# Output projection and gate of a hybrid decoder layer as seven quadrant products per pair of token tiles

## The chip, the cores and the metric

One core of a Trainium2 chip. The metric is the device time of one execution in microseconds; given is the median of three runs. The profile is of one further execution. TensorE (PE) does the matrix products, VectorE (DVE), ScalarE (ACT) and GpSimd (POOL) everything else; SyncE (SP) and the queue of ACT issue the transfers. Each engine works off its own instructions in program order.

## The reference

One decoder layer over 2048 prompt tokens and 8 x 8 sample tokens, width 1024, all in float32:

```
h   = rms_norm(x) ; z = h @ w_in                       # 1024 -> 3584
a   = silu(gate_A) * u * (W_s layernorm(v) + b)        # spatial gating, 512 wide
b   = silu(gate_B) * groupnorm(retention(q, k, v))     # 4 heads, 512 wide
mix = concat(a, b) @ w_out                             # 1024 -> 1024
x   = x + rms_norm(mix)
x   = x + sigmoid(x @ w_gate) * (p @ w_ple)            # 1024 -> 1024, 256 -> 1024
```

It returns the new x of both token sets, the retention states and the normalised v rows of the sample.

## The kernel before

The prompt is 16 tiles of 128 tokens, the sample one tile of 64. The work runs in five passes over these 17 tiles (sample between tiles 7 and 8): S (u, v and gate of the spatial part, three groups of 512 columns), R twice (two heads each: q and k, then v and gate), C1 (the output projection, two groups of 512 columns) and C2 (the gate, two groups of 512, each followed by the embedding product of the same columns). A main product has 128 features by 128 tokens stationary and 128 by 512 of a weight moving. For float32 accuracy each operand is split into a rounded part (hi) and its remainder (lo), and each chunk of 128 features costs three products, hi-hi, hi-lo and lo-hi; for the sample hi and lo lie side by side in the stationary operand and it costs two. So a C1 tile has 2 x 8 x 3 = 48 main products and a C2 tile 48 + 2 x 2 x 3 = 60.

`Stream` (L53) writes the order of every engine out by hand. It counts the main products issued. After each one `tick()` runs the closures that fall due and steps the generators of side work: a `yield 4` in one means that its next instruction is written down four products later. Where a text says that something stands at product n, it means this place in the program; the engine reaches it when what stands ahead of it on that engine is done.

`weight_pass` and `fill` (L199, L232) load, round (ACT, L214 or L216) and subtract (DVE, L223 or L225) the weights; hi and lo stay in the pool `ring`, 52 slots of 2 KB. The operands of a tile are split by `split_cols` (L242: ACT L251, then DVE or POOL L253) and lie in the pool `big`, ten buffers of 4 KB. Further pools hold the temporaries. A pool gives out again the slot that has been free longest; the first writer waits for the last user of the slot.

Between the passes the activations go through DRAM: a tile is transposed in blocks of 32 by 32 on DVE (`blocks`, L176) and scattered (`scatter`, L183) to `mixT` and `x2T`, from which the next pass loads features by tokens, in runs of 1 KB. In C1 (`post`, L801) two squares on ACT with a sum (L807) give the norm, three small POOL operations its factor (L811, L295, L296), DVE scales straight out of PSUM (L818), POOL adds the residual (L822), and the ACT queue issues the store of x2 and the four parts of its transposed form, five issues a tile. In C2 (L835, L841) ACT takes the tanh of the gate out of PSUM (L838) and DVE combines it with the embedding product, in PSUM too, and with x2 (L850, L853). The main products use four PSUM banks of 512 columns in turn, the side products four others.

In R, POOL rotates q and k (L474, L475, L478), multiplies the gate with the group-norm weights (L504) and works on the group norm (L535 to L537, L546).

Of the kernel before, what the change touches and what calls it, by code (L numbers as in the profile page):

```python
# [12 lines left out]
F32 = mybir.dt.float32  # L13
# [36 lines left out]
F_0 = 10  # L50


class Stream:  # L53
    """Orders the tensor engine: main products, with side work placed between them."""
# [50 lines left out]
def hybrid_step(ctx: ExitStack, tc: tile.TileContext, a: dict):  # L105
# [4 lines left out]
    ring = ctx.enter_context(tc.tile_pool(name="ring", bufs=52))  # L110
    big = ctx.enter_context(tc.tile_pool(name="big", bufs=10))
# [10 lines left out]

    def wtile(shape, dt=F32):
        return ring.tile(shape, dt, tag="W", name=name("W"))

    def vtile(shape, dt=F32):
        return work.tile(shape, dt, tag="v2", name=name("v2"), bufs=8)

    def xtile(shape, dt=F32):
        return big.tile(shape, dt, tag="X", name=name("X"))  # L130

    def t2k(shape, dt=F32):
        return work.tile(shape, dt, tag="t2", name=name("t2"), bufs=10)

    def t1k(shape, dt=F32):
        return work.tile(shape, dt, tag="t1", name=name("t1"), bufs=11)

    def c4k(shape, dt=F32):
        return work.tile(shape, dt, tag="c4", name=name("c4"), bufs=2)
# [27 lines left out]
    x2T = [dram.tile([4 if t < NT else 2, P, KD, 32], F32, name=f"x2T{t}") for t in range(NT + 1)]  # L167
    x2d = [dram.tile([P if t < NT else TS, D], F32, name=f"x2d{t}") for t in range(NT + 1)]
# [7 lines left out]
    def blocks(tile_, src, n):  # L176
        """src [n, 128 * nk] transposed in blocks of 32 by 32, the blocks of one quarter of the features together"""
# [5 lines left out]
    def scatter(dst, src, n, qu=None):  # L183
        """src [n, 4, nk, 32] from blocks() to dst [n / 32, 128, nk, 32] in DRAM: features by tokens"""
# [9 lines left out]
    def mm(out, l, r, start, stop):  # L194
        st.pe = True
        PE.matmul(out, lhsT=l, rhs=r, start=start, stop=stop)  # L196
# [44 lines left out]
    # ------------------------------------------------------- x operands (split)  # L241
    def split_cols(raw, t, eng):  # L242
# [6 lines left out]
        if len(raw.shape) == 4:  # L249
            hi, lo = (o.rearrange("p k (a r) -> p a k r", r=32) for o in (hi, lo))  # L250
# [647 lines left out]
    def length(u):  # L898
        if u.first:
            return 216  # L900
# [178 lines left out]
```

## Time and profile before

| | |
|---|---|
| median of 3 runs | 1148.37 us (1147.71 to 1148.89) |
| span of the profiled execution, first to last instruction | 1146.2 us |
| PE busy | 1139.0 us, 99% |
| DVE, ACT, POOL busy | 53%, 30%, 38% |
| mean transfer rate | 138 GB/s |

The profile gives for the profiled execution its span; the runs are timed from outside and their median lies 2.2 us above it. Busy time of PE is the time covered by its records, which overlap each other at their ends.

### The profile page before, as it was taken

What the parts mean: (1) busy time and instruction counts of PE and PEld (TensorE: products, weight loads), DVE (VectorE), ACT (ScalarE), POOL (GpSimd) and SP (SyncE); (2) the same over time, 40 slices, a digit from 0 to 9 for tenths busy, and PEclk for the clock granted to TensorE, in tenths of its full rate; (3) what the DMA queues carried; (4) which work ended last, traced back from release to release, by engine and by line L of the source; (5) the groups of instructions that cost most, each with busy time, mean ns of one, the idle gap of its engine ahead of it and who ended that gap; (6) DMA issues with size and microseconds to landing.
All of it is one profiled execution on the core that took longest, in us unless ns stands there. A gap on an engine that the chain in (4) does not pass through costs nothing.

```text
span 1146.2 us, 15123 instructions
## 1 busy us (share of the span) xinstructions
PE 1139.0 (99%) x5316; PEld 943.1 (82%) x5316; DVE 604.7 (53%) x1094; ACT 346.5 (30%) x648; POOL 436.3 (38%) x621
## 2 busy tenths in 40 slices
PE   9999999999999999999999999999999999999998
PEld 7888878888888888788888887888888888888886
DVE  4866575566745655675456457643344652233332
ACT  6543433335312322242123123412222421112110
POOL 6654434533334465653444575443334210000000
PEclk9999999999999999999999999999999999999999
DMA  9343123124353442663443427656666763335431
GB/s 312 98 146 96 40 73 119 39 85 135 101 159 96 119 110 81 189 184 97 117 121 95 117 70 213 212 193 191 202 228 227 240 221 120 108 111 150 131 106 55
DMA packets 140300, 157.75 MB, mean 138 GB/s; under 512 B 30656, under 2 KB 106688, under 8 KB 140224
## 3 DMA queue, kind: packets, MB, share of 16 engines
q1 hardware_dynamic: 128336, 139.48, 39.9%
q10 hardware_dynamic: 11888, 17.31, 4.8%
q8 instruction: 42, 0.69, 0.3%
q14 instruction: 34, 0.28, 0.1%
HBM read 110.99 MB, written 45.74 MB: 137 GB/s over the span
## 4 chain that ended last, share of the span: by engine, by line
PE 94%; DMA 2%; POOL 2%; DVE 1%; SPq 1%; issue 0%; ACT 0%; DVEq 0%; ACTq 0%; POOLq 0%
PE z L196 87%; PE s L196 7%; DMA W<-w_in 1%; DMA X<-x 1%; POOL v L377 1%; POOL t L361 0%; SPq L920 0%; DMA X<-sguT 0%; POOL X L253 0%; SPq L207 0%; DVE ti L351 0%; DVE t L337 0%; DVE t L333 0%; DVE W L225 0%; DVE X L305 0%
## 5 line engine op out<-in xcount | busy, mean ns | idle before, releaser
L196 PE MATMUL z<-W,X 128*128 128x512 f32 x4328 | 1072.6, 396 | 1.6 <-DVE W L225 0.8
L196 PEld LDWEIGHTS z<-W,X 128*128 128x128 f32 x4328 | 804.0, 188 | 164.4 <-issue 2.6
L253 DVE TENSOR_TENSOR X<-X,X 128x1024 fp32r<-128x1024 f32 (+1 forms) x68 | 81.1, 1192 | 36.6 <-PE z L196 16.4
L850 DVE SCALAR_TENSOR_TENSOR t<-t,z 128x512 f32<-128x512 f32 (+1 forms) x33 | 22.2, 672 | 142.1 <-PE z L196 142.1
L251 ACT CAST X<-X 128x1024 fp32r<-128x1024 f32 (+1 forms) x82 | 83.7, 1020 | 32.9 <-issue 22.8
L196 PEld LDWEIGHTS s<-t,t 128*128 128x128 f32 (+1 forms) x400 | 73.6, 186 | 13.1 <-issue 3.1
L196 PE MATMUL s<-t,t 128*128 128x128 f32 (+2 forms) x400 | 76.3, 272 | 0.0
L498 ACT ACTIVATE t<-z,rsall 128x256 f32<-128x256 f32 x32 | 15.2, 476 | 196.4 <-PE z L196 191.9
L180 DVE STREAM_TRANSPOSE t<-t 128x256 f32<-128x256 f32 (+3 forms) x69 | 39.8, 577 | 61.5 <-POOL t L478 42.5
L838 ACT ACTIVATE t<-z 128x512 f32<-128x512 f32 x32 | 19.1, 598 | 170.5 <-PE z L196 167.6
L474 POOL TENSOR_TENSOR t<-t,t 128x256 f32<-128x256 f32 (+1 forms) x34 | 27.3, 802 | 100.4 <-DVE t L471 86.3
L225 DVE SCALAR_TENSOR_TENSOR W<-W,c_npre,W 128x512 fp32r<-128x512 f32 x56 | 44.7, 819 | 19.9 <-ACT W L216 19.8
L822 POOL TENSOR_TENSOR X<-X,t 128x512 f32<-128x512 f32 (+1 forms) x34 | 45.7, 1364 | 18.1 <-DVE t L818 12.0
L196 PE MATMUL z<-W,t 128*128 128x512 f32 x200 | 50.9, 389 | 0.0
L535 POOL TENSOR_TENSOR ti<-ti,c_cols 128x2 f32<-128x2 f32 (+1 forms) x34 | 11.2, 328 | 96.1 <-DVE ti L531 96.1
L504 POOL TENSOR_TENSOR t<-t,gnw 128x256 f32<-128x256 f32 (+1 forms) x34 | 40.1, 1178 | 18.8 <-DVE t L502 18.4
L216 ACT ACTIVATE W<-W,c_npre 128x512 fp32r<-128x512 f32 x56 | 39.1, 719 | 25.7 <-DMA W<-w_in 23.4
L807 ACT ACTIVATE t<-z 128x512 f32<-128x512 f32 x32 | 19.1, 598 | 91.1 <-PE z L196 91.1
L196 PEld LDWEIGHTS z<-W,t 128*128 128x128 f32 x200 | 37.5, 188 | 7.8
L529 DVE BATCH_NORM_STATS2 ti<-s 128x6 f32<-128x128 f32 x64 | 15.8, 288 | 50.3 <-PE s L196 50.3
L377 POOL TENSOR_TENSOR v<-t,v 128x128 fp32r<-128x128 f32 x64 | 31.4, 512 | 23.4 <-ACT v L375 17.7
L253 POOL TENSOR_TENSOR X<-X,X 128x1024 fp32r<-128x1024 f32 (+1 forms) x14 | 32.9, 2353 | 15.7 <-ACT X L251 9.6
(118 smaller groups left out, 1042.5 us busy)
## 6 DMA issues: line engine op xcount, KB each, us to landing
X<-xT SPq DMA_DIRECT2D x45, 512.0 KB, 4.0
X<-x SPq DMA_DIRECT2D x32, 512.0 KB, 5.0
W<-w_in SPq DMA_DIRECT2D x56, 256.0 KB, 4.4
qkT<-t SPq DMA_DIRECT2D x132, 64.0 KB, 2.0
x2T<-c ACTq DMA_DIRECT2D x66, 128.0 KB, 2.6
t<-qkT SPq DMA_DIRECT2D x32, 256.0 KB, 3.0
X<-mixT SPq DMA_DIRECT2D x16, 512.0 KB, 4.4
x2d<-X ACTq DMA_DIRECT2D x16, 512.0 KB, 2.7
```

Of the source, the lines that this page charges most:

```text
L180: V.transpose(out=out.rearrange("p b k r -> p k b r"), in_=src.rearrange("p (k b r) -> p k b r", b=4, r=32))
L196: PE.matmul(out, lhsT=l, rhs=r, start=start, stop=stop)
L216: S.activation(out=hi, in_=raw, func=AF.Copy, scale=sc)
L225: V.scalar_tensor_tensor(out=lo, in0=raw, scalar=sc, in1=f(hi), op0=ALU.mult, op1=ALU.subtract)
L251: S.copy(out=hi, in_=raw)
L253: eng.tensor_tensor(out=lo, in0=raw, in1=f(hi), op=ALU.subtract)
L377: GP.tensor_tensor(out=los[q][:, :, t % 4, :], in0=i, in1=f(o), op=ALU.subtract)
L474: GP.tensor_tensor(out=qk[:, :, 0, :], in0=t1[:, :, 0, :], in1=t2[:, :, 1, :], op=ALU.subtract)
L504: GP.tensor_tensor(out=g, in0=g, in1=ret["gn"][0:n, 256 * pr : 256 * pr + 256], op=ALU.mult)
L807: S.activation(out=junk, in_=src, func=AF.Square, accum_out=acc["a"][:, g : g + 1])
L822: GP.tensor_tensor(out=x2[:, c], in0=x2[:, c], in1=w, op=ALU.add)
L850: V.scalar_tensor_tensor(out=th[g][:, h], in0=th[g][:, h], scalar=1.0, in1=src[:, h], op0=ALU.add, op1=ALU.mult)
```

## The change

C1 and the gate of C2 no longer work tile by tile. `Fast` takes a pair of token tiles as two block rows and halves features and columns. The left operand has the quadrants A11, A12 (first tile, features 0 to 511 and 512 to 1023), A21, A22 (second tile), the weight B11 to B22. Seven products of quadrants, each of 4 chunks by 3 products, give the four results (Winograd's form of Strassen's scheme), 84 main products for what took 96. The sample tile stays with 32 products, from weights that are there (B12 is B11 + T1, so it adds two products).

Each weight now has 28 chunks of hi and lo, 56 slots, in place of 32. Sixteen of the 28 are differences made on POOL (T1 and T3 of two loaded chunks, T2 and T4 of a loaded chunk and the difference before); they are formed in place in the raw chunk, rounded on ACT and subtracted on DVE. POOL makes four sums of operands (S1 to S4) per pair. Products 1, 3 and 5 add into one PSUM bank ("a"), 2 and 4 into another ("c"), and ACT copies the contents out between them; DVE adds the parts.

The embedding product no longer stands beside the gate: `Ple` is a pass of its own between C1 and C2 that writes its result to DRAM (`pleD`), and C2 reads it back. In C1 the sample is last, in C2 first.

Temporaries, weights and operands share one ring of 98 slots of 2 KB; every 4 KB tile is now two of 2 KB, with two loads or operations for one. So the transposed tiles move in runs of 512 B (1 KB before), those of the spatial part in runs of 256 B (512 B before). The pool of 1 KB tiles grows from 11 to 14. The scratch that the program sets aside for descriptors shrinks to 1 KB.

```diff
-    ring = ctx.enter_context(tc.tile_pool(name="ring", bufs=52))
-    big = ctx.enter_context(tc.tile_pool(name="big", bufs=10))
+    ring = ctx.enter_context(tc.tile_pool(name="ring", bufs=SLOTS))     # 98
...
+    PRODUCTS = (("A11", "B11", "a"), ("S1", "T1", "c"), ("S2", "T2", "a"), ("S4", "B22", "c"),
+                ("S3", "T3", "a"), ("A22", "T4", "d"), ("A12", "B21", "b"))
...
+        def combine(dst, x, y, op):
+            GP.tensor_tensor(out=raws[dst], in0=raws[x], in1=raws[y], op=op)
+        for k in range(4):
+            job("B11", k, lambda k=k: raws[0, 0, k], [(0, 0, k)])
+        for k in range(4):
+            job("T1", k, lambda k=k: raws[0, 0, k], [(0, 1, k)],
+                lambda k=k: combine((0, 0, k), (0, 1, k), (0, 0, k), ALU.subtract))
...                                    # T2 the same way; B22 alone; T3, T4 as T1; B21 alone
+    def fast_fill(jobs, counts):
+        for (loads, scales, total, high, low), c in zip(jobs, counts):
+            for fn in loads:
+                st.at(c - 8 - LAG_W, fn)
...
+            if total:
+                st.at(c - 7, total)
+            st.at(c, high)
+            st.at(c + 4, low)
...
+        def total(self, x, y, op):
+            out = slot("sum", [P, 4, 4, 32])
+            GP.tensor_tensor(out=out, in0=x, in1=y, op=op)
+            return out
+        def prep(self):                                   # from 44 products ahead of the pair
...
+            s1 = self.total(r[1, 0], r[1, 1], ALU.add)
+            yield from self.split("A11", r[0, 0])         # ACT rounds, 4 products later DVE subtracts
+            yield 4
+            s2 = self.total(s1, r[0, 0], ALU.subtract)
+            yield 4
+            yield from self.split("S1", s1)
+            s4 = self.total(r[0, 1], s2, ALU.subtract)
+            yield 8
+            yield from self.split("S2", s2)
+            s3 = self.total(r[0, 0], r[1, 0], ALU.subtract)
+            yield 8
...                                                       # S4, S3, A22, A12, 8 products apart
+        def after(self, i, banks):
...
+            if i == 0:
+                copy("m1", "a")                           # ACT, PSUM to SBUF
+            elif i == 1:
+                copy("m5", "c")
+            elif i == 2:
+                copy("u2", "a")
+            elif i == 3:
+                add("u2", "c")                            # DVE, PSUM + SBUF
+                st.start(self.post_(t0, 1, c["u2"]), 3)
+            elif i == 4:
+                copy("u3", "a")
+                add("m5", "a")
+                st.start(self.post_(t1, 1, c["m5"]), 3)
+            elif i == 5:
+                add("u3", "d")
+                st.start(self.post_(t1, 0, c["u3"]), 3)
+            else:
+                add("m1", "b")
+                st.start(self.post_(t0, 0, c["m1"]), 3)
...
+    class Ple:                                            # 12 products a tile, 8 for the sample
...
+                out = slot("P", [P, 512])
+                S.copy(out=out, in_=bank)
+            store(pleD[self.t][:, 512 * g : 512 * g + 512], out[0:n])
...
+    unitsC1 = [Fast(p, tabC1, mixT, c1_post, c1_begin) for p in pairs + [[SAMPLE]]]
+    unitsP = [Ple(t, PleTab()) for t in order]
+    unitsC2 = [Fast(p, tabC2, x2T, c2_post, c2_begin) for p in [[SAMPLE]] + pairs]
...
+        last = begin[unitsR[1][-1]]
+        fast_fill(jobsC1, [last - 10 * (14 - j) for j in range(14)] + [last + 4 + 7 * j for j in range(14)])
+        fill(stepsP, [begin[unitsC1[-1]] + 4 + 6 * j for j in range(4)])
+        last = begin[unitsC1[-2]]
+        fast_fill(jobsC2, [last + 50 + 8 * j for j in range(28)])
...
+            if isinstance(u, Fast):
+                lead = 84, 44                             # products from load, from prep, to the pair
+            elif isinstance(u, Ple):
+                lead = 48, 16
```

The steps behind a result stay in kind: in C1 squares, norm, scaling by DVE (now in place, out of SBUF), the residual on POOL, then the store of x2 and the scatter of its transposed form in halves, ten issues a tile on the ACT queue; in C2 the tanh on ACT (SBUF to SBUF), then the two DVE operations with the embedding result and x2 from SBUF.

## Rows read from the trace of the kernel before

**Rows 1.** The page, part 1: busy us, share, instructions.
```profile
PE 1139.0 (99%) x5316; PEld 943.1 (82%) x5316; DVE 604.7 (53%) x1094; ACT 346.5 (30%) x648; POOL 436.3 (38%) x621
```

**Rows 2.** Windows: R, C1, C2; busy us (instructions), granted clock, DMA share, GB/s.
```profile
core 0: us, PE busy (x) PEld busy (x) DVE busy (x) ACT busy (x) POOL busy (x), PEclk, DMA share, GB/s
...
330.00:754.00 424.00, 424.00 (x2102) 352.80 (x2100) 245.40 (x554) 115.40 (x213) 219.09 (x294) 1.00 0.46 131
754.00:927.00 173.00, 173.00 (x766) 143.35 (x766) 81.39 (x97) 49.63 (x102) 62.40 (x84) 1.00 0.69 221
927.00:1146.00 219.00, 214.63 (x947) 177.43 (x946) 70.03 (x103) 40.01 (x67) 0.00 (x0) 1.00 0.37 119
```

**Rows 3.** Timeline of PE in C2: start us, length us, group.
```profile
1010.00 5.60 PE L196 MATMUL z<-W,X 128*128 128x512 f32 x24
1015.44 1.52 PE L196 MATMUL z<-W,t 128*128 128x512 f32 x6
1016.80 5.60 PE L196 MATMUL z<-W,X 128*128 128x512 f32 x24
```

**Rows 4.** Groups by shape, 754 to 1146 us: busy us, mean ns | idle before.
```profile
L822 POOL TENSOR_TENSOR X<-X,t 128x512 f32<-128x512 f32 x30 | 40.2, 1361 | 17.0 <-DVE t L818 11.8 <-issue 5.2
...
L253 DVE TENSOR_TENSOR X<-X,X 128x1024 fp32r<-128x1024 f32 x29 | 35.5, 1223 | 34.5 <-PE z L196 16.4 <-ACT X L251 13.1 <-DMA x2d<-X 5.0
...
L818 DVE SCALAR_TENSOR_TENSOR t<-z,ti,c 128x512 f32<-128x512 f32 x30 | 21.4, 745 | 17.5 <-POOL ti L296 17.5
...
L838 ACT ACTIVATE t<-z 128x512 f32<-128x512 f32 x32 | 19.1, 598 | 170.5 <-PE z L196 167.6 <-DMA x2T<-c 2.9
L180 DVE STREAM_TRANSPOSE c<-X 128x1024 f32<-128x1024 f32 x15 | 18.7, 1244 | 23.0 <-POOL X L822 22.3 <-DMA x2T<-c 0.7
...
L214 ACT CAST W<-W 128x512 fp32r<-128x512 f32 x20 | 11.9, 617 | 11.2 <-DMA W<-w_ple 4.1 <-POOL X L822 3.1 <-DMA W<-w_gate 1.8
L296 POOL TENSOR_TENSOR ti<-ti,nhalf 128x1 f32<-128x1 f32 x15 | 8.6, 571 | 1.3
...
L747 ACT CAST t<-t 128x256 fp32r<-128x256 f32 x16 | 6.4, 399 | 3.1 <-DMA x2T<-c 2.9 <-issue 0.2
L807 ACT ACTIVATION_READ_ACCUMULATOR t<-z 128x1 f32 x29 | 5.6, 194 | 0.0
```

**Rows 5.** Timeline of ACT around the start of C1; ACTq is its queue issuing.
```profile
736.23 0.60 ACT L807 ACTIVATE t<-z 128x512 f32<-128x512 f32 x1 [4.51 <-PE z L196]
...
755.41 0.60 ACT L807 ACTIVATE t<-z 128x512 f32<-128x512 f32 x1 [1.79 <-PE z L196]
755.42 0.84 ACTq L187 DMA_DIRECT2D x2T<-c  x2
...
763.71 1.90 ACTq L187 DMA_DIRECT2D x2T<-c  x3
```

**Rows 6.** Timeline of POOL at the end of R.
```profile
717.84 0.20 POOL L535 TENSOR_TENSOR ti<-ti,c_cols 128x2 f32<-128x2 f32 x1 [2.72 <-DVE ti L531]
...
720.66 0.73 POOL L504 TENSOR_TENSOR t<-t,gnw 128x256 f32<-128x256 f32 x1
721.60 1.05 POOL L546 TENSOR_TENSOR t<-t,t 128x256 f32<-128x256 f32 x1 [0.21 <-DVE t L541]
725.43 1.11 POOL L474 TENSOR_TENSOR t<-t,t 128x256 f32<-128x256 f32 x1 [2.78 <-DVE t L471]
...
727.77 0.95 POOL L478 TENSOR_TENSOR t<-t,c_cols 128x256 f32<-128x256 f32 x1
730.74 0.56 POOL L535 TENSOR_TENSOR ti<-ti,c_cols 128x2 f32<-128x2 f32 x1 [2.02 <-DVE ti L531]
...
733.86 0.73 POOL L546 TENSOR_TENSOR t<-t,t 128x256 f32<-128x256 f32 x1 [0.20 <-issue]
```

**Rows 7.** Timeline of all engines at the end.
```profile
1141.73 0.42 DVE L850 SCALAR_TENSOR_TENSOR t<-t,z 128x256 f32<-128x256 f32 x1 [5.38 <-PE z L196]
...
1142.98 0.42 DVE L853 SCALAR_TENSOR_TENSOR X<-t,X 128x256 f32<-128x256 f32 x1
```

**Rows 8.** Groups by shape on POOL, whole kernel.
```profile
L504 POOL TENSOR_TENSOR t<-t,gnw 128x256 f32<-128x256 f32 x32 | 38.6, 1206 | 13.7 <-DVE t L502 13.3 <-DMA qkT<-t 0.3
```

More of the change, by code (lines that the diff above doesn't have):

```diff
@@ L167, in hybrid_step @@
     x2T = [dram.tile([4 if t < NT else 2, P, KD, 32], F32, name=f"x2T{t}") for t in range(NT + 1)]
+    pleD = [dram.tile([P if t < NT else TS, D], F32, name=f"ple{t}") for t in range(NT + 1)]
     x2d = [dram.tile([P if t < NT else TS, D], F32, name=f"x2d{t}") for t in range(NT + 1)]
@@ new lines, in hybrid_step, with c2_begin, c2_post @@
+    c2 = {}
+    def c2_begin(tiles):
+        for t in tiles:
+            for g in (1, 0):
+                for what, src in (("ple", pleD), ("x2", x2d)):
+                    tl = slot(what, [P, 512])[0 : np_(t)]
+                    SY.dma_start(out=tl, in_=src[t][:, 512 * g : 512 * g + 512])
+                    c2[what, t, g] = tl
+    def c2_post(t, g, src):
+        n = np_(t)
+        th = src[0:n]
+        S.activation(out=th, in_=th, func=AF.Tanh, scale=0.5)
+        yield 4
+        ple, x2 = c2.pop(("ple", t, g)), c2.pop(("x2", t, g))
+        w = 256 if t == 14 and g == 0 else 512
+        for o in range(0, 512, w):
+            h, c = slice(o, o + w), slice(512 * g + o, 512 * g + o + w)
+            V.scalar_tensor_tensor(out=th[:, h], in0=th[:, h], scalar=1.0, in1=ple[:, h], op0=ALU.add, op1=ALU.mult)
+            V.scalar_tensor_tensor(out=x2[:, h], in0=th[:, h], scalar=0.5, in1=x2[:, h], op0=ALU.mult, op1=ALU.add)
+            store((a["o_ys"] if t == SAMPLE else a["o_y"][t])[:, c], x2[:, h])
@@ L870, in hybrid_step @@
     order = list(range(8)) + [SAMPLE] + list(range(8, NT))
+    pairs = [[2 * j, 2 * j + 1] for j in range(NT // 2)]
     tabS, fillS = weight_pass(in_specs([1, 0, 2]))
@@ L914, in hybrid_step @@
         for t in u0.tiles:
-            u0.ops[t] = (xtile([P, KD, P], F32R), xtile([P, KD, P], F32R))
+            u0.ops[t] = [(slot("A", [P, 4, P], F32R), slot("A", [P, 4, P], F32R)) for _ in range(2)]
         def x_part(t, q):
@@ new lines, in hybrid_step, with ret_gn @@
+        fill(stepsR[1], first8(us[-3]) + [begin[us[-1]] + 6 + 6 * j for j in range(8)])
+        last = begin[unitsR[1][-1]]
[3 more added lines that the diff above has]
+        fast_fill(jobsC2, [last + 50 + 8 * j for j in range(28)])
+        def ret_gn():
+            ret["gn"] = work.tile([P, 512], F32, tag="lc", name="gnw", bufs=1)
+            SY.dma_start(out=ret["gn"], in_=a["ret_gn"])
@@ L973, in hybrid_step @@
+        for i, u in enumerate(units):
             assert st.count == begin[u]
+            if isinstance(u, Unit) and i:
+                st.finish(u.prepping)
             u.begin()
```

543 lines of the change are left out of this document (343 added, 200 removed).

## The prediction

> **What bounds the kernel now.** I read the page first, then the stages by windows, the tensor engine's timeline in one stage, and the groups by shape. The tensor engine is busy in 99% of the span [rows 1], and in R, C1 and C2 its busy time equals the stage's length, at full granted clock, but for the last 4 us [rows 2]. So a product removed there is worth its pitch, as long as nothing else starts to make the engine wait. The pitch: a C2 group of 24 gate products and its 6 embedding products follow each other every 6.80 us [rows 3], 6.80 / 30 = 0.2267 us. (Records of neighbours overlap, so the 389 ns of one is not the pitch.) The other engines are far from full in C1: DVE 47%, ACT 29%, POOL 36%, DMA 69% [rows 2]. They do matter because each works in program order: an instruction that waits holds up all behind it.
>
> **What is removed.** C1 and C2 now have 16 x (48 + 60) + 32 + 40 = 1800 main products. After: C1 8 x 84 + 32 = 704, embedding 16 x 12 + 8 = 200, C2 704, together 1608. 192 products fewer x 0.2267 = **43.5 us**. Shapes are unchanged (128 columns stationary, 512 moving), so I keep the pitch. That is the whole gain; everything below is a cost.
>
> **Steady C1, per pair.** A pair lasts 84 x 0.2267 = 19.0 us. From [rows 4], halving what is priced at 1024 elements: POOL 4 sums and 4 residual adds at 1.36 us, and twice the three small operations of the norm, of which the power takes 0.57 us and the other two less, about 2.2 us: 13.1 us. DVE 7 subtracts at 0.61 to 0.69, 4 additions from PSUM and 4 scalings at 0.75, 4 transposes at 0.62: 13.1 us. ACT 7 roundings at 0.62, 4 copies out of PSUM at 0.60, 4 squares at 0.60 + 0.19: 9.9 us, and 20 DMA issues (now 10 per two tiles) at about 0.42: 8.4 us. [Rows 5] show two issues of 0.84 us in all running under a square that began 0.01 us earlier, so the issues lie beside the arithmetic unless they wait: ACT is nearer 10 than 18 us. DMA bytes per token stay in C1 (2 MB a tile); 0.69 x 21.8 us is 15 us per two tiles, less when the gate weights move to later; runs of 512 B in place of 1 KB could add what R pays per byte over C1, (0.46/131) / (0.69/221) = 1.13 [rows 2], so at most 17 of 19 us, and its loads have 84 products (19 us) of lead. All are under 19.0 us.
>
> What could make TensorE wait is bank "a": products 1, 3 and 5 add into it, and ACT must have copied it in between. The cover is the product between, 12 x 0.2267 = 2.7 us, against a copy of 0.6. ACT's thick stretch is between products 28 and 56 of a pair: 18 issues, 7.6 us of them, in 6.3 us, so it runs one to two us late, and recovers before the next copies. I take 1 us in all for C1 and C2 together, between 0 and 8 (0.5 us a pair).
>
> Slots: counted from the allocations and last uses, a steady C1 pair holds at most 58 lasting ones (56 weights, 2 of the norm) and 29 others, 87 of 98. With 11 free and about 38 taken per pair, a slot is some 5 us old when it is taken again. I cost that at nothing; at the end of R the count comes to about 92, and a wait there could cost up to 3 us, which goes into the range.
>
> **The first pair: the largest cost.** The C1 weights need 16 POOL differences. Eight (T1, T2) fall in the three units before R's last one, eight (T3, T4) between products 11 and 60 after that unit begins; the first pair's four operand sums fall between 4 and 32. R keeps POOL busy 52% meanwhile [rows 2]. Times in the old trace: the first square of C1 starts at 736.23 [rows 5], 24 products after C1 begins, so C1 begins near 730.3; R's normalisations start at 717.84 and 730.74 [rows 6], a unit is 12.9 us and the last one begins near 717.4. POOL's queue from 717.8, in program order: normalisation to 722.65 (4.8 us), six sums (8.2), the rotation 725.43 to 728.72 (3.3), four sums (5.4), the next normalisation 730.74 to 734.59 (3.8), one more sum (1.4): 26.9 us, so T4's third chunk is ready near 744.7. Its rounding stands on ACT at product 60, one ahead of the copy of the first product out of bank "a" at 61; so the copy ends near 746, and TensorE wants the bank back 24 products after 730.3, plus 0.3 of side products, at 736. This gives 10 us of waiting. Part of the POOL blocks is waiting and stretching that sums would fill, so I take **8 us**; bounds 0 (all covered) and, with the sums stretched as below, 18. The R products that wait for ACT (v, the transposed q and k) are held by the same roundings at the same time and are not added.
>
> T1 and T2 in R: a difference is queued 7 products (1.9 us) ahead of its rounding and takes 1.36 us when POOL is free; behind a normalisation the rounding, and with it the copy of q and k behind it, is late by up to 4 us with some 2 us of cover. **1 us**, 0 to 4.
>
> **Embedding pass and C2 weights.** 200 products, 45.3 us. ACT: 16.5 tiles x (0.40 + 2 x 0.60) [rows 4] = 26.3 us, 19 roundings of C2 weights 11.7 us, together 38 us, and C1's last 17 issues, 7.1 us, in the first 24 products (5.4 us). It is close to full but four banks let TensorE run three groups, 3 x 6 x 0.2267 = 4.1 us, ahead of the copies. **1 us**, 0 to 6. The weight differences, 16 x 1.36 us = 22 us, have POOL almost to themselves. C2: no POOL adds and no ACT issues; only the four sums, DVE near 13 us. Loads of the embedding result and of x2 start with the pair and have 48 products, 11 us.
>
> **The end.** Now, after the last product, two operations in two halves, the last starting at 1142.98 [rows 7]. After: first an addition from PSUM (0.75) and the tanh (0.60), with two hand-overs of about 0.1 us: **1.6 us** more (1.3 to 2.5).
>
> **S and R otherwise.** Halved loads, squares and splits add instructions, not work for TensorE: per S tile about 0.4 us on POOL and ACT and 6 more issues on SP in 16 us. Covered; 0, with up to 2 us in the range.
>
> **Sum.** The span is 1146.2 and the median of the runs 1148.4; 2.2 us lie outside the records, and I leave them as they are. 1148.4 - 43.5 + 1 (steady) + 8 (first pair) + 1 (end of R) + 1 (embedding) + 1.6 (end) = 1117.5, say **1118 us**.
>
> **A rule that speaks against it.** POOL's price is not fixed. [Rows 6 and 8]: one line's multiply of 128 x 256 takes 0.73 us at 720.66 and 1.21 us on the mean of 32, 1.65 times. In C1, DVE would rise from 47% to 69%, most of it with two SBUF inputs. The Trainium skill, "GPSIMD Engine Reference", section Specifications, says that POOL's SBUF interfaces are shared with VectorE, and that DVE instructions with two SBUF inputs contend; its section on engine selection advises against POOL for two-input elementwise work. The stretch in the rows agrees with that.
>
> **Rivals.**
> 1. *Nothing waits at the first pair.* If POOL's sums fill R's gaps (it is idle 48% there), only the end costs: 1148.4 - 43.5 + 1.6 = 1106.5, say 1107. For it: sums are asked for 80 products ahead. Against: eight differences and four sums in 56 products. 0.15.
> 2. *POOL becomes the bound of C1.* At 1.65 times, 8 x 1.36 x 1.65 + 2.2 x 1.3 = 20.8 us per pair against 19.0: 8 x 1.8 = 14 us, and the first pair 2 us worse: about 1133. The point where it decides is a mean sum of 2.0 us. Against: POOL's adds in C1 stand at 1.36 [rows 4], with DVE at 47%. 0.15.
> 3. *Slower: copies out of bank "a" late in all 16 pairs.* If ACT's copy ends 5.6 us after its product rather than 0.8, TensorE waits 2.9 us per pair: 16 x 2.9 = 46, 1107 + 46 = 1153. The point is 2.7 us per pair, a copy 5.4 us after its product. For it: an issue that waits for POOL or DVE does hold up ACT (three issues took 1.90 us, [rows 5]). Against: C2 has no such issue, and C1's have 12 products (2.7 us) from the producer to the issue. 0.06.
>
> The forecast case, waits of 5 to 20 us in all, has 0.64, with its own range 1110 to 1125.
>
> **Numbers.** A difference under 0.2% (2.3 us) can't be told from no change here. The range reaches down to rival 1 and up to rival 2: 1106 to 1133; some 0.2 is outside, most of it above. Faster 0.93 (forecast, rivals 1 and 2, less 0.02 for costs that add up), same 0.01, slower 0.06.
>
> **What would show it.** 192 fewer main products at 0.227 us; C1 after its first pair at 19 us per pair; one gap of TensorE of several us within the first 36 products of C1, released by ACT, which stands behind a rounding that waits for a POOL sum; POOL sums at 1.3 to 1.5 us. I am wrong if gaps return in every pair, if POOL's sums take 2 us or more, if the embedding pass is well over 46 us, or if the granted clock leaves 1.00.

## The result and the profile after

The changed kernel is slower: 1161.8 us (median of 4 runs, 1159.5 to 1162.9) against 1148.3 on the same chip, a ratio of 1.0114 [1.0099, 1.0128]. The forecast was 1118 us, with a range up to 1133.

The page of the changed kernel, part 1 and the clock line of part 2, beside [rows 1]:

```profile
PE 1115.5 (96%) x5124; PEld 915.1 (79%) x5124; DVE 774.8 (67%) x1353; ACT 451.4 (39%) x935; POOL 578.8 (50%) x748
...
PEclk9999999999989999999999999899999989999999
```

The 192 products are gone (5316 to 5124), and yet the span grew from 1146.2 to 1159.9 us: TensorE now stands idle for 44 us of it and has slices below full clock, which it had not before. The windows say where (transition from S to R, start of C1, the other pairs of C1, embedding pass, C2; the columns are those of [rows 2]):

```profile
310.00:345.00 35.00, 29.58 (x132) 24.48 (x132) 16.28 (x38) 6.06 (x12) 8.58 (x13) 0.90 0.46 115
738.00:775.00 37.00, 29.22 (x134) 24.40 (x133) 30.36 (x51) 18.14 (x39) 27.48 (x28) 0.86 0.48 140
775.00:930.00 155.00, 143.26 (x604) 114.29 (x603) 119.24 (x145) 66.98 (x144) 100.95 (x102) 0.98 0.70 211
930.00:993.67 63.67, 53.79 (x208) 40.66 (x209) 51.04 (x64) 39.71 (x82) 37.41 (x29) 0.92 0.75 242
993.67:1153.40 159.73, 159.73 (x705) 131.99 (x703) 112.04 (x155) 69.72 (x123) 41.17 (x28) 1.00 0.63 209
```

C2 is what was forecast: no idle time, clock 1.00, 704 products in 159.73 us, 0.2269 us each, beside 0.2267 in [rows 3]. Every loss lies before it. TensorE's timeline, the idle time and its releaser in brackets:

```profile
339.04 0.80 PE L196 MATMUL s<-t 128*128 128x128 f32 x2 [5.42 <-ACT t L511]
...
751.84 0.79 PE L196 MATMUL s<-t 128*128 128x128 f32 x2 [7.78 <-ACT t L511]
...
787.57 12.79 PE L196 MATMUL z<-W,A 128*128 128x512 f32 x48 [3.62 <-ACT C L893]
...
829.75 10.49 PE L196 MATMUL z<-W,A 128*128 128x512 f32 x45 [1.10 <-ACT C L893]
...
932.31 3.42 PE L196 MATMUL z<-W,A 128*128 128x512 f32 x8 [3.47 <-DVE C L930]
935.56 0.63 PE L196 MATMUL z<-W,t 128*128 128x512 f32 x2
937.70 1.42 PE L196 MATMUL z<-W,t 128*128 128x512 f32 x5 [1.51 <-DVE t L1016]
```

All 20 gaps of over 0.2 us behind the first microseconds add up to 36.6 us: 5.4 where R begins, 1.9 at R's end, 7.8 at the first pair of C1, 3.6 in the second, 6.9 in the six pairs after it (0.4 to 1.8 each), 11.1 at C1's end and in the embedding pass. In the second to the eighth pair the gap stands in the middle, ahead of main product 48: there the fifth of the seven quadrant products begins to add into bank "a", out of which ACT must have copied the third.

Behind the longer gaps the granted clock is at 0.50, the 1.2 GHz level, for 3.4 to 10.2 us; before the kernel's last microseconds these stretches add up to 34.1 us. They begin in part while TensorE still stands idle; it was busy in 26.5 us of them and does half the work in these, so the half clock cost at most 13 us more. 36.6 + 13 is some 50; the profiled execution (1161.7) is 55.2 above the sum without any wait, 1148.4 - 43.5 + 1.6 = 1106.5. The last 5 us lie in neither and are not placed.

**The queues of S to R and of C1.** SP's timeline where S ends; every group is issues:

```profile
313.91 2.67 SPq L186 DMA_DIRECT2D mixT<-t  x6
...
317.12 4.77 SPq L186 DMA_DIRECT2D mixT<-t  x10
...
323.37 6.90 SPq L186 DMA_DIRECT2D mixT<-t  x12
...
330.78 1.87 SPq L186 DMA_DIRECT2D mixT<-t  x4
332.70 1.39 SPq L186 DMA_DIRECT2D qkT<-t  x3
335.52 0.38 SPq L508 DMA_DIRECT2D t<-qkT  x1
```

The same results went out in 16 issues before, each with twice the bytes; now they are 32 of 0.45 to 0.58 us, and the stores of R's transposed q and k stand behind them. In the kernel before the last of these stores and the load of them read:

```profile
324.94 2.07 SPq L187 DMA_DIRECT2D qkT<-t  x3
328.56 0.38 SPq L486 DMA_DIRECT2D t<-qkT  x1
```

The load (now L508) begins at 335.52 where it began at 328.56. It follows the last store's issue by 1.4 us now and by 1.6 us then, so it is not the shorter runs of the transfers that make it late but its place in the queue. ACT's copy of it (L511) is late with it, and the scores at 339.04 wait 5.4 us.

ACT's timeline at the first pair and at a later one; ACTq is its queue issuing:

```profile
745.56 0.62 ACT L745 CAST W<-wraw 128x512 fp32r<-128x512 f32 x1 [3.92 <-POOL wraw L757]
...
748.46 0.62 ACT L745 CAST W<-wraw 128x512 fp32r<-128x512 f32 x1 [1.76 <-POOL wraw L757]
...
751.17 0.61 ACT L511 COPY t<-t 128x512 f32<-128x512 f32 x1
753.14 0.62 ACT L745 CAST W<-wraw 128x512 fp32r<-128x512 f32 x1 [1.35 <-POOL wraw L757]
753.66 0.58 ACT L893 COPY C<-z 128x512 f32<-128x512 f32 x1
...
829.11 0.58 ACT L893 COPY C<-z 128x512 f32<-128x512 f32 x1 [3.03 <-DMA x2T<-t]
829.13 0.86 ACTq L186 DMA_DIRECT2D x2T<-t  x2
830.04 0.62 ACT L815 CAST A<-X 128x512 fp32r<-128x512 f32 x1 [0.34 <-issue]
830.06 3.90 ACTq L186 DMA_DIRECT2D x2T<-t  x8
834.05 0.62 ACT L815 CAST A<-sum 128x512 fp32r<-128x512 f32 x1 [3.40 <-DMA x2T<-t]
```

At the first pair ACT's roundings (L745) wait for POOL's differences, as forecast; but the first thing to stand behind them is R's copy of q and k (L511), whose two score products TensorE meets 18 main products into C1, before it needs bank "a" again. The later pair begins at 817.19, so the third quadrant product, 36 main products on, is through near 825.4. Its copy out of bank "a" starts only at 829.11, after three microseconds without arithmetic on ACT: four issues stood in front of it and waited for POOL's residual additions, the last of which ended at 828.63. TensorE, at main product 48, waits 1.1 us for this copy. At 830.06 eight more issues hold up the next rounding by 3.4 us.

**POOL and DVE.** Groups by shape, 740 us to the end:

```profile
L983 POOL TENSOR_TENSOR X<-X,C 128x512 f32<-128x512 f32 x32 | 47.7, 1491 | 15.6 <-DVE C L981 15.6
...
L757 POOL TENSOR_TENSOR wraw<-wraw,wraw 128x512 f32<-128x512 f32 x22 | 33.8, 1547 | 14.0 <-DMA wraw<-w_gate 13.7 <-DVE t L1016 0.4
...
L981 DVE SCALAR_TENSOR_TENSOR C<-C,ti,npost 128x512 f32<-128x512 f32 x32 | 46.2, 1446 | 6.6 <-POOL ti L305 6.6
L896 DVE TENSOR_TENSOR C<-z,C 128x512 f32<-128x512 f32 x64 | 43.8, 685 | 16.6 <-ACT C L893 8.4 <-PE z L196 8.2
...
L179 DVE STREAM_TRANSPOSE t<-X 128x512 f32<-128x512 f32 x32 | 21.7, 691 | 0.2 <-POOL X L983 0.2
```

The scaling L981 is costed at 0.745 us from [rows 4], where it read PSUM. Now both its inputs lie in SBUF and it takes 1.45. The addition with one input in PSUM (L896) and the transpose with one input (L179) keep 0.69. POOL's sums and differences stand at about 1.5, the upper end of what was forecast. The Trainium skill, "GPSIMD Engine Reference", section Specifications, names DVE instructions with two SBUF inputs among those that contend with POOL. The trace agrees: L981 takes 0.75 us at 819.13, with POOL idle, and 1.78 at 820.40, beside one of POOL's additions.

### The profile page after: what moved, and what is told of

The parts are those of the page before. It is cut to its first block, busy times and chain, and to the rows that moved or that the text cites. A ratio compares the mean times of both kernels' runs of the same rounds, so it can differ in the third digit from the quotient of the medians.

```text
span 1159.9 us, 16198 instructions
## 1 busy us (share of the span) xinstructions
PE 1115.5 (96%) x5124; PEld 915.1 (79%) x5124; DVE 774.8 (67%) x1353; ACT 451.4 (39%) x935; POOL 578.8 (50%) x748
## 4 chain that ended last, share of the span: by engine, by line
PE 73%; POOL 7%; DVE 6%; DMA 5%; issue 3%; ACT 3%; SPq 1%; ACTq 1%; POOLq 0%; DVEq 0%
PE z L196 67%; PE s L196 6%; POOL X L983 3%; DMA x2T<-t 2%; DVE W L750 1%; DMA X<-x 1%; POOL wraw L757 1%; DVE C L896 1%; ACTq L186 1%; ACT A L815 1%; POOL sum L822 1%; DVE C L981 1%; ACT C L893 1%; ACT t L970 0%; DMA W<-w_in 0%
## 5 line engine op out<-in xcount | busy, mean ns | idle before, releaser
L196 PE MATMUL z<-W,A 128*128 128x512 f32 x4136 | 1036.4, 399 | 14.2 <-ACT C L893 10.5
L196 PEld LDWEIGHTS z<-W,A 128*128 128x128 f32 x4136 | 773.6, 190 | 175.1 <-ACT C L893 15.1
L822 POOL TENSOR_TENSOR sum<-X,X 128x512 f32<-128x512 f32 x32 | 45.6, 1424 | 100.5 <-DMA X<-x2T 92.2
L179 DVE STREAM_TRANSPOSE t<-t 128x256 f32<-128x256 f32 (+3 forms) x69 | 39.8, 577 | 61.7 <-POOL t L500 39.3
L817 DVE TENSOR_TENSOR A<-X,A 128x512 fp32r<-128x512 f32 (+1 forms) x52 | 49.3, 948 | 37.4 <-ACT A L815 35.9
L893 ACT COPY C<-z 128x512 f32<-128x512 f32 x64 | 37.5, 586 | 93.6 <-PE z L196 51.2
L750 DVE TENSOR_TENSOR W<-wraw,W 128x512 fp32r<-128x512 f32 x56 | 57.0, 1020 | 10.5 <-ACT W L745 9.0
L254 ACT CAST A<-X 128x512 fp32r<-128x512 f32 (+1 forms) x96 | 57.7, 603 | 7.4 <-DMA X<-xT 7.3
L983 POOL TENSOR_TENSOR X<-X,C 128x512 f32<-128x512 f32 (+1 forms) x34 | 50.9, 1497 | 18.3 <-DVE C L981 17.2
L817 DVE TENSOR_TENSOR A<-sum,A 128x512 fp32r<-128x512 f32 x64 | 47.5, 743 | 15.3 <-ACT A L815 14.7
L745 ACT CAST W<-wraw 128x512 fp32r<-128x512 f32 x56 | 34.5, 622 | 52.6 <-POOL wraw L757 45.8
L896 DVE TENSOR_TENSOR C<-z,C 128x512 f32<-128x512 f32 x64 | 43.8, 685 | 16.6 <-ACT C L893 8.4
L757 POOL TENSOR_TENSOR wraw<-wraw,wraw 128x512 f32<-128x512 f32 x32 | 47.5, 1493 | 14.0 <-DMA wraw<-w_gate 13.7
L981 DVE SCALAR_TENSOR_TENSOR C<-C,ti,npost 128x512 f32<-128x512 f32 (+1 forms) x34 | 47.7, 1404 | 6.6 <-POOL ti L305 6.6
```

The costliest lines, as they stand in the source:

```text
L179: V.transpose(out=out.rearrange("p b k r -> p k b r"), in_=src.rearrange("p (k b r) -> p k b r", b=4, r=32))
L196: PE.matmul(out, lhsT=l, rhs=r, start=start, stop=stop, skip_group_check=again)
L254: S.copy(out=hi, in_=r)
L750: V.tensor_tensor(out=lo, in0=raw(), in1=f(cell[0]), op=ALU.subtract)
L757: GP.tensor_tensor(out=raws[dst], in0=raws[x], in1=raws[y], op=op)
L817: V.tensor_tensor(out=lo, in0=raw, in1=f(hi), op=ALU.subtract)
```

## Experiments

Each base is named; all are measured against the kernel before on the same chip (1147.9 to 1148.2 us). A difference between two kernels compares medians of different chips where they ran on different ones; the kernel before differs by up to 0.5 us between these. "Base" from the second section on is the changed kernel with the first two edits. In kernels with the first edit lines stand 4 lower in the file: L893 is L897 there.

### Transfers: one scatter in S, C1's issues off ACT

In `s_post` both halves are transposed into one tile of 2 KB and scattered once, in runs of 512 B:

```diff
-                for c in range(2):
-                    bt = blocks(t1k([P, 256]), us[h][c][:, i, :], P)
-                    scatter(mixT[...][:, :, 2 * c : 2 * c + 2, :], bt, P)
+                bt = t2k([P, 512])...
+                for c in range(2):
+                    V.transpose(out=bt[:, :, 2 * c : 2 * c + 2, :]..., in_=us[h][c][:, i, :]...)
+                scatter(mixT[...][:, :, 0:4, :], bt, P)
```

> The spatial part's two transposed halves of a tile go into one 2 KB tile and leave in four transfers in runs of 512 B, as before the change, in place of eight in runs of 256 B. Theory (SP's queue): at the end of S the 32 issues of the last four tiles, 0.43 us each, stand ahead of the first R tile's round trip of q and k; TensorE stood still for 5.4 us at 339 and then ran at half clock for 6.8 us. With 16 issues the gap and the half clock go: 9 us less, 1153 us. Rival (the ring of slots is short): the slots stay as they are, no change, 1162 us.

1153.5 us, 1.0049 [1.0034, 1.0064]: 8.3 less, as expected. The gap of 5.4 and its 6.8 us of half clock are gone; TensorE had been busy in 5.6 of these, so 5.4 + 2.8 = 8.2 were to be had.

C1's stores and scatters issued by SP:

```diff
-            store(x2d[t][:, 512 * j : 512 * j + 512], x2[j], S)
+            store(x2d[t][:, 512 * j : 512 * j + 512], x2[j])
...
-            scatter(x2T[t][:, :, 4 * j : 4 * j + 4, :], bt, n, S)
+            scatter(x2T[t][:, :, 4 * j : 4 * j + 4, :], bt, n)
```

> The 20 issues per C1 pair that store x2 and its transposed form go to SP in place of ACT. Theory (ACT is late with its copies out of PSUM because 3.9 us of issues stand ahead of them): the gap of 1.1 us at the start of each C1 pair goes, and part of the embedding pass's waits, 8 to 10 us less, near 1153 us. Rival (POOL and DVE set the pair): the gaps stay, within 2 us of 1162.

1147.1 us, 0.9993 [0.9983, 1.0002]: 14.7 less, more than expected (and the waits it removes stand at main product 48 of a pair, not at its start). TensorE's groups by shape in that kernel (main products, scores of R):

```profile
L196 PE MATMUL z<-W,A 128*128 128x512 f32 x3017 | 763.7, 400 | 6.4 <-DVE C L930 6.4
...
L196 PE MATMUL s<-t 128*128 128x128 f32 x128 | 26.0, 286 | 14.7 <-ACT t L511 14.7
```

No main product waits for ACT's copy any more (10.5 us before this edit), and the half clock behind the wait of 3.6 us is gone too; what waits for R's copies is untouched. The Trainium skill, "DMA: Bandwidth & Descriptors", section "Issuing engines are not separate DMA queues", says that issuing from several engines saves only the time of issuing. Here the same transfers from another engine are worth 14.7 us, because of what stands behind an issue that waits.

Both together:

> Both changes to transfers together: the spatial part's scatter in four issues a tile, and x2 with its transposed form issued by SP. Theory (two separate queues, SP at the end of S, ACT in C1): the gains of 8.4 and 14.7 us add, 1138.5 us, faster than the kernel before by 9 us; what is left against the ideal of 1107 us are the first C1 pair and the start of the embedding pass. Rival (SP gets too full when it has both): less than the sum, 1142 us or more.

1139.1 us, 0.9925 [0.991, 0.994]: 22.7 less, the sum of the two. C1 from the last wait in its first pair to the next wait, in the sample tile, by windows:

```profile
759.43:903.20 143.77, 143.77 (x640) 118.86 (x638) 122.26 (x151) 65.80 (x143) 105.52 (x105) 1.00 0.75 220
```

Steady C1 runs without a wait at full clock, with DVE 85% and POOL 73% busy. POOL was not the bound of C1.

### The ring

`SLOTS = 94` in the changed kernel, for 98.

> The changed kernel with 94 slots in the ring in place of 98, nothing else. Theory (queues and shared interface): the slots are not what waits, the same as the changed kernel, 1160 to 1164 us. Rival (the ring of slots is short, and waits for slots make the gaps): four slots fewer make it slower by 5 us or more, 1167 us or more.

1161.1 us, 1.012 [1.0103, 1.0137]: no change that can be told. Slots aren't what is waited for.

### The differences

All 32 differences of the weights on DVE (changed kernel), then the operands' sums as well:

```diff
-            GP.tensor_tensor(out=raws[dst], in0=raws[x], in1=raws[y], op=op)
+            V.tensor_tensor(out=raws[dst], in0=raws[x], in1=raws[y], op=op)
...                                                        # second kernel, in total():
-            GP.tensor_tensor(out=out, in0=x, in1=y, op=op)
+            V.tensor_tensor(out=out, in0=x, in1=y, op=op)
```

> The weight differences T1 to T4 are made on DVE in place of POOL. Theory (POOL's queue, stretched by the SBUF interface that it shares with DVE): a difference takes 0.65 to 0.75 us in place of 1.3 to 1.75, nothing of the weights stands on POOL, the gap of 7.8 us at the first pair shrinks to 0 to 3 us and the embedding pass loses most of its gaps: 15 to 25 us less, near 1141 us. Rival (it is DVE's work that is too much, at the end of R and in the embedding pass): DVE gets 32 more operations, the gaps stay or grow, 1160 to 1175 us.

> As the run with the differences on DVE, and the operand sums S1 to S4 on DVE too; POOL keeps only the residual additions. Theory (shared interface): what POOL gives up costs DVE half, the gap of 1.1 us at the start of every C1 pair shrinks, 5 us less than with the differences alone, near 1136 us. Rival (DVE's work): DVE has 16 of 19 us per pair, pairs get longer, 0 to 10 us more than with the differences alone.

1155.7 (1.0068 [1.0053, 1.0083]) and 1156.4 (1.0078 [1.0061, 1.0095]): 6 less each, where 20 and 25 were expected. The gap at the first pair is still 5.4 and 4.1 us; the later pairs' gaps stay in the first kernel and are two a pair (about 0.7 and 1.1) in the second. The theory of that moment, that POOL alone was behind most of the loss, fell here.

What the differences cost at the first pair was then measured without them. This kernel is the base with the sixteen differences of C1's weights left out: the raw chunks are rounded as they are, so C1 multiplies by other weights, with the same number of products.

```diff
+    jobsC1 = [(l, s, None, h, w) for l, s, _, h, w in jobsC1]
```

> The kernel with one scatter per group and C1's stores on SP (1139.1 us), with the sixteen differences of C1's weights left out: the raw chunks are rounded as they are, so C1 multiplies by other weights; the number of products, copies and roundings stays. Theory: ACT stands in front of R's last q/k copies and of the copy out of bank a because its roundings wait for the differences on POOL. Then the gap of 7.78 us at the first pair falls below 2 us and its 6.8 us of half clock goes: 1139.1 - 6 - 3.4, about 1130 (1127 to 1133). Rival: R's own tail is what is late there, and the differences only happen to stand beside it: gap stays above 5 us, 1136 to 1139.

1128.5 us, 0.983 [0.9816, 0.9845]: 10.5 less than the base. ACT's timeline there, and below it the copy of q and k (L515) in the base:

```profile
732.06 0.61 ACT L515 COPY t<-t 128x512 f32<-128x512 f32 x1
732.58 0.61 ACT L749 CAST W<-wraw 128x512 fp32r<-128x512 f32 x1
733.10 0.58 ACT L897 COPY C<-z 128x512 f32<-128x512 f32 x1
```

```profile
743.22 0.61 ACT L515 COPY t<-t 128x512 f32<-128x512 f32 x1
```

The copy that ended at 743.8 in the base now ends at 732.7. The gap of 7.8 us is gone and one of 1.35 stands in its place, at a copy out of a bank; the half clock is gone too, and so are the 1.9 us at R's end. The differences are the cause, through ACT's queue. Two milder edits: every second one on DVE, and the last 16 chunks rounded later.

```diff
-            GP.tensor_tensor(out=raws[dst], ...)
+            (V if both and dst[2] % 2 else GP).tensor_tensor(out=raws[dst], ...)
...                                                        # the other kernel:
-        fast_fill(jobsC1, [...] + [last + 4 + 7 * j for j in range(14)])
+        fast_fill(jobsC1, [...] + [last + 34 + 6 * j for j in range(14)])
```

> The base (one scatter per group and C1's stores on SP, 1139.1 us), with every second of C1's sixteen weight differences on DVE and the others on POOL. Theory: POOL was overloaded in R's last units (its own work there plus a difference per 10 products), so with half of them on the engine beside it neither falls behind, and the gap of 7.78 us at the first pair falls under 4 us: 1130 to 1135. Rival: a difference takes DVE as long as POOL and stretches both, as when all of them were moved: gap of 5 us or more, 1136 to 1139.

> The base (1139.1 us) with the last 16 of C1's 28 weight chunks (B22, T3, T4, B21) rounded at products 34, 40, ... after R's last unit begins in place of 4, 11, ...: the roundings that wait for a difference then stand behind R's last q/k copies. Theory (POOL's differences hold up ACT, and through it the copies): the gap of 7.78 us falls below 3 us and its half clock goes, 1127 to 1133. Rival: the work does not fit between there and its use, so the sixth and seventh product of the first pair wait in its place: 1136 to 1140.

1136.8 (0.9904 [0.9889, 0.9918]) and 1137.2 (0.9908 [0.9893, 0.9922]): some 2 us each, at the rivals' end. The gap goes to 6.1 and 4.7. On DVE a difference of C1's weights takes 1.12 us in the first kernel (0.93 with all on DVE) and POOL's go from 1.39 to 1.51: moving half of them stretches both. In the second, three of the eight T3 and T4 still stand ahead of the copy; the first of their roundings waits 5.8 us for POOL, to 734.6.

### C1's end and the embedding pass

Base, three edits: the sample first in C1 (B21 is split before T3 and T4 for it), or the gate's weights 36 products later, and to that a longer lead for the embedding's operands.

```diff
-    unitsC1 = [Fast(p, ...) for p in pairs + [[SAMPLE]]]
+    unitsC1 = [Fast(p, ...) for p in [[SAMPLE]] + pairs]
...                                                        # second and third
-        fast_fill(jobsC2, [last + 50 + 8 * j for j in range(28)])
+        fast_fill(jobsC2, [last + 86 + 8 * j for j in range(28)])
...                                                        # third
-                lead = 48, 16
+                lead = 60, 32
```

> As the run with both transfer changes, and the sample tile first in C1 (it needs only B11, T1, B22 and B21, and B21 is split before T3 and T4), so that T3 and T4 are wanted 32 products, 7 us, later and the sample's work stands no longer between C1 and the embedding pass. Theory (POOL's differences are late for ACT at the first pair, and the embedding pass starts on a crowd): the first gap of 7.8 us becomes 3 or less with its half clock, the gaps after C1 lose about half: 1138 - 10 = 1128 us. Rival (the order of POOL, ACT and DVE is the same whatever the tile, so the wait for R's last products, which ACT's roundings hold up, stays): 1136 to 1140 us.

> As the run with both transfer changes, and the gate's weights 36 products later each, so that their first differences fall into the embedding pass and not on the last C1 pair and the sample. Theory (the gaps around 918 to 945 us come from those differences, stretched on POOL and DVE, ahead of the sample's copies on ACT): 5 to 8 us less than that run, near 1132 us. Rival (it is the sum of work on DVE there, 48 of 55 us, that is too much): the gaps move into the embedding pass, the same time within 2 us.

> The base with the gate's weights 36 products later (1136.6 us), and the embedding pass's operands loaded 60 and split 32 products ahead of their group in place of 48 and 16. Theory: the gaps there that end on the subtraction of the embedding operand (some 4 us in all) are a matter of lead, since the subtraction stands on DVE behind weights and transposes; with 3.6 us more of lead they go, and some of the 10.2 us of half clock with them: 1129 to 1133. Rival: DVE and ACT are full there, so the wait only goes to another instruction: 1135 to 1138.

1137.1 (0.9905 [0.989, 0.9919]), 1136.6 (0.9904 [0.9877, 0.9932]) and 1137.0 (0.989 [0.9859, 0.9921]). The first mostly moved the waits: the 7.8 and 6.7 us became 5.5 for ACT's copy at the first pair and smaller ones, of 0.4 to 3.4 us, at C1's start and in the embedding pass. In the second the wait of 6.7 us at C1's end is gone, as its theory had it (no gap there is over 2.0 us in the profile). But its four runs lie at 1133.8, 1134.4, 1138.8 and 1140.8 us, those of the third at 1132.1, 1134.2, 1139.7 and 1140.6: two groups each, so the medians say little, and the third can't be told from the second. The profile of the third is of the run of 1140.6. POOL, then DVE:

```profile
927.47 10.34 POOL L761 TENSOR_TENSOR wraw<-wraw,wraw 128x512 f32<-128x512 f32 x8
...
925.04 5.50 DVE L754 TENSOR_TENSOR W<-wraw,W 128x512 fp32r<-128x512 f32 x1
930.47 7.62 DVE L1020 TENSOR_TENSOR t<-t,t 128x256 fp32r<-128x256 f32 x1
938.02 0.69 DVE L179 STREAM_TRANSPOSE t<-X 64x512 f32<-64x512 f32 x1
```

While POOL works off eight differences in a row, 1.29 us each, a DVE subtraction that takes 0.41 us a moment later takes 7.6: DVE does not get in until POOL pauses, and TensorE waits 6.1 us for that subtraction. The profile of the second is of the run of 1133.8, with the same eight in a row:

```profile
926.46 12.35 POOL L761 TENSOR_TENSOR wraw<-wraw,wraw 128x512 f32<-128x512 f32 x8
...
932.75 1.78 DVE L754 TENSOR_TENSOR W<-wraw,W 128x512 fp32r<-128x512 f32 x1
934.45 1.51 DVE L1020 TENSOR_TENSOR t<-t,t 128x256 fp32r<-128x256 f32 x1
```

There POOL takes 1.54 us for each and DVE's subtractions get in between, at 1.8 us at most. So two engines that contend shared in one execution and did not in the other. This fits the two groups of runs, with one profile from each; what decides between them stays open.

### The clock

Base with 24 main products more into a spare bank, their result unused. The first kernel puts them right before the third quadrant product of the first pair (after 24 main products), the second after the sixteenth main product. The code is the second's:

```diff
+        def fill_up(self):
+            bank = zbank()
+            for m in range(24):
+                mm(bank, self.ops["S1"][0][:, m % 4, :], self.tab["T1", 0][0], m == 0, m == 23, False)
...
+            if self.filler:
+                seq[15] = (seq[15][0], self.fill_up)
```

> The same base (1139.1 us) with 24 more products, 5.4 us, put into a spare PSUM bank right before the third product of the first pair, where TensorE stands idle for 7.78 us; their result is not used. Theory: the granted clock falls to half because TensorE had stood idle, so with the gap cut to about 2.4 us the 6.8 us of half clock there do not come: 1139.1 - 3.4, about 1135.7 (1134.5 to 1137). Rival: the clock falls for another reason, or after the shorter gap as well: 1138.5 to 1140.

> The base (1139.1 us) with 24 more products, 5.4 us, into a spare bank after the sixteenth product of the first pair, ahead of the two side products that wait 7.78 us there; their result is not used. The earlier try stood behind them. Theory: the gap shrinks to 2.3 us and TensorE's clock stays at full speed, so 6.8 to 10.2 us of half clock go: 1139.1 - 3.4 to 5.1, about 1135 (1134 to 1136.5), though more products are done. Rival: the clock falls all the same: 1138.5 to 1140.

The first: 1143.5 us, 0.9962 [0.9949, 0.9975]. Neither expectation held: the products stood behind R's scores, which are what waits, so the gap stayed (7.9), and they cost 4.4 of their 5.4 us. The second: 1137.7 us, 0.991 [0.9896, 0.9925], no slower than the base with 24 products more. Windows behind the gap in the base and in this kernel:

```profile
743.88:749.00 5.12, 5.12 (x19) 4.38 (x20) 4.43 (x6) 1.39 (x3) 5.12 (x6) 0.67 0.04 9
```

```profile
743.43:752.00 8.57, 7.66 (x37) 5.88 (x38) 7.87 (x12) 3.95 (x9) 6.49 (x6) 1.00 0.13 32
```

With the gap at 2.4 us the clock stays at 1.00. But neither expectation was met. The theory's 3.4 us are half of 6.8 us; TensorE had been busy in only 3.4 of these, so 1.7 was the most to be had. And what it gained there it waited for again, in part at two copies out of bank "a" (0.4 and 0.5 us): R's next scores began at 758.3 in place of 758.7. Here the half clock was a consequence of the gap, and with ACT late anyway it cost little; at the transition from S to R it seems to have cost its whole half (8.3 measured, 8.2 by the sum above).

### Towards a better version

The edits combined: every second difference of C1 on DVE, with C1's late chunks and the later gate's weights; the same with the sample first, without the late chunks; then the embedding's stores on ACT; then the gate's weights loaded 30 products earlier.

```diff
-            store(pleD[self.t][:, 512 * g : 512 * g + 512], out[0:n])
+            store(pleD[self.t][:, 512 * g : 512 * g + 512], out[0:n], S)
...
-                st.at(c - 8 - LAG_W, fn)
+                st.at(c - 8 - LAG_W - early, fn)                # 30 for the gate's, 0 for C1's
```

> The same, with C1's last 16 weight chunks rounded from product 34 on (4 before) and the gate's weights 36 products later. Theory: the gains add: 1139.1 - 5 (engine) - 2 (C1's chunks) - 2.5 (gate's), 1128 to 1132. Rival: late chunks take back what the others give: 1133 to 1137.

> The kernel with C1's sample tile first (1137.1 us), with every second of C1's differences on DVE and the gate's weights 36 products later. Theory: at C1's end the sample's additions no longer stand behind the last pair, and the gate's weights are out of the way, so the gaps of the embedding pass (9 us, with 10.2 us of half clock) mostly go, and the first pair's shrink: 1125 to 1130. Rival: the sample at the start needs B21 and so pushes T3 and T4 behind the first pair's use: 1132 to 1137.

> The version with the sample first (1130.9 us), with the stores of the embedding pass's result issued by ACT, right behind its own copy, in place of SP. Theory: SP issues without a pause there (x2's scatters, the stores and the gate's weights), so the weights land late, POOL's differences wait for them, and ACT's roundings for those: with 34 issues less on SP the gaps of 1.7, 1.7 and 0.4 us at the end of the pass go, and half clock with them: 1126 to 1129. Rival: 34 issues of 0.4 us are more than ACT has room for there, and its copies come late: 1130 to 1135.

> The same, with the gate's weights loaded 30 products, 6.8 us, earlier. Theory (the weights' loads are late on SP): another 1 to 3 us, 1124 to 1128. Rival: the loads then stand in front of C1's last scatters and stores, which nothing waits for, so nothing more is won than by the stores: as the run before, within 1 us.

1130.5 (0.9862 [0.9833, 0.9891]; three runs at 1130.2 to 1130.6 and one at 1137.5, the profiled one, in which POOL again has eight differences in a row and a DVE subtraction takes 7.3 us), 1130.9 (0.9849 [0.9833, 0.9866]), 1133.7 (0.9877 [0.9864, 0.9891]) and **1128.1** (0.9825 [0.9812, 0.9839]). The first came out as expected, the second 1 us above its range. The stores on ACT cost rather than gained, as the rival had it; with earlier loads they go with the best version, 5.6 us below the run before it, where 1 to 3 were expected. POOL's differences of the gate's weights in these two, the earlier loads second:

```profile
L761 POOL TENSOR_TENSOR wraw<-wraw,wraw 128x512 f32<-128x512 f32 x16 | 24.8, 1572 | 10.8 <-DMA wraw<-w_gate 10.8
```

```profile
L761 POOL TENSOR_TENSOR wraw<-wraw,wraw 128x512 f32<-128x512 f32 x16 | 24.5, 1550 | 3.1 <-DVE W L754 1.9 <-DMA wraw<-w_gate 1.2
```

So the weights did land late: POOL waited 10.8 us for them and now waits 1.2. In the changed kernel too its first difference for the gate, at 921.02, waits for a load that SP issued at 917.98 and that landed at 920.80. The page of the best version:

```profile
PE 1104.6 (98%) x5124; PEld 910.5 (81%) x5124; DVE 783.7 (70%) x1361; ACT 449.8 (40%) x935; POOL 577.5 (51%) x740
...
PEclk9999999999999999999999999999999989999999
```

It beats the kernel before by 20 us, with the same products as the changed one. It still has 13.8 us of gaps from R's start on and 10.2 us of half clock ahead of the kernel's end. The earlier loads weren't tried with the stores on SP.

## Why the prediction was wrong

**Right.** The removed 43.5 us: pitch and count are as forecast, and C2 shows them bare. C2 without a wait, POOL not the bound of C1, no lack of slots. End of R 1.9 us (forecast 1, at most 4). The end: 1159.9 - 1153.4 = 6.5 us after the last product, 4.6 before, so 1.9 where 1.6 was taken. The mechanism of the first pair: roundings that wait for POOL's differences hold up ACT, and TensorE with it.

**Sizes off.** *The first pair*, 8 us with bounds 0 and 18, and 1 us at R's end: C1's differences cost 10.5 together. The first thing late was the copy of q and k, which the prediction named and did not add because it is held by the same roundings; it was right not to add it, and wrong that TensorE would first wait for bank "a". *The embedding pass*, 1 us with at most 6: 200 products that last 45.3 us took 58. With the end of C1 it holds 11.1 us of gaps and 10.2 us of half clock, with TensorE busy in 8.2 of these, so some 15 us together. The working asked whether ACT fits in; what TensorE waited for was DVE in every one of these gaps, and DVE had no term. It was busy 51 of 64 us there, and its subtractions and scalings of 128 x 512 with both inputs in SBUF stood at 1.0 to 1.3 us and not at 0.61 to 0.75. The stretch had been looked for in POOL alone, and there it was small. Behind DVE stood a second thing without a term, gate weights that SP loads late. How the 15 us divide between the two is not shown.

**Steps that failed.** *"S and R otherwise ... 6 more issues on SP in 16 us. Covered; 0"*: 8.3 us. The sum of issues was compared with the time of an S tile; what counts is what stands behind the last of them in the queue. *"The issues lie beside the arithmetic unless they wait"*, and ACT "runs one to two us late, and recovers before the next copies", with 1 us for the pairs: 14.7 us. The condition was stated and then dropped, and one copy does not come after the thick stretch, between products 28 and 56: the third quadrant product's copy out of bank "a" stands in it, at product 37. Issues for a result that POOL and DVE had not made yet kept ACT from it, with twenty issues a pair in place of ten. *The granted clock at 1.00 throughout*, which had no term: up to 13 us, all behind gaps.

**The signs and the rivals.** Of the four signs of being wrong that the prediction gave, three came: gaps in every pair of C1, an embedding pass well over 46 us, a clock below 1.00. Rival 3, slower by late copies out of bank "a", has its mechanism in C1: issues that hold up ACT. Its price was wrong: 0.4 to 1.8 us in six pairs and 3.6 in the second, none in C2, not 2.9 in sixteen. That the time ended near its 1153 and beyond comes from a sum over four places, each of which had been called covered or small, or priced too low. Rival 2 asked for sums of 2.0 us on POOL and saw 1.5. Rival 1 was nowhere near: even the best version, after seven edits of order and engines, stands 21 us above 1107. The chances for "faster" add to 0.92 (0.64 + 0.15 + 0.15 - 0.02), not 0.93.

Not settled: how the half clock's 13 us divide between time lost and time that would have been waited in any case; only two places were measured.

## What to carry to other kernels

When TensorE sets the end alone, a change that removes products is worth its pitch only if every in-order queue beside it keeps its order of arrival: for each engine and each transfer queue, list what stands *behind* an instruction that waits, and not only how full the queue is. Halving a tile doubles issues, and the first user behind a burst of issues pays for all of them. Where POOL and DVE work at once, cost DVE's instructions with two SBUF inputs at what such an instruction takes beside POOL.

## What the runs showed of the hardware

- DVE's instructions with two SBUF inputs and POOL's sums hold each other up: POOL's 128 x 512 sums take 1.29 us alone and some 1.7 beside DVE, DVE's subtractions 0.68 alone and up to 1.8 beside POOL. Against a row of eight of POOL's a DVE subtraction of 0.41 us took 7.6 in one execution; in another such a row took 12.35 us in place of 10.34 and DVE got in between. Additions with one input in PSUM and transposes were not stretched (0.69).
- After gaps of TensorE the granted clock was 0.50 for 3.4 to 10.2 us, in part of which TensorE was still idle; with the same gap shortened from 7.8 to 2.4 us it stayed at 1.00.
- The same issues of transfers, about 0.4 us each, cost 14.7 us less on SP's queue than on ACT's, where arithmetic stood behind them.
